# Gate modulation moved under the FFN, attention results in tiles of their own, two FFN result tiles

## The chip, the cores and the metric

The kernel runs on one core of a Trainium2 chip, in one launch. The metric is the device time of that launch in microseconds. Each number given as the kernel's time is the median of several executions. The engines are named as in the profile: PE (TensorE, matrix products), PEld (its weight loads), DVE (VectorE), ACT (ScalarE), POOL (GpSimd) and SP (SyncE, which here only issues DMA transfers). POOL and ACT issue DMA transfers too. Every engine works through its own instruction list in order.

## What is computed

One layer of an encoder, for 512 tokens of 2048 features, in float32:

```python
mod = silu(c) @ w_ada + b_ada                 # c is one row; w_ada is 2048 x 12288
sh1, sc1, g1, sh2, sc2, g2 = split(mod, 6)
h = rms_norm(x, norm1_w) * (1 + sc1) + sh1
qa, ka, va, qb, kb, vb, ga, gb = split(h @ w_in)
ya = global_gqa(rope(rms(qa)), rope(rms(ka)), va)     # 8 heads of 128
yb = neighbourhood_attention(qb, kb, vb, rpb)         # 8 heads of 128
merged = sigmoid(ga) * (ya @ w_oa) + sigmoid(gb) * (yb @ w_ob)
x = x + g1 * (merged @ w_out)
h2 = rms_norm(x, norm2_w) * (1 + sc2) + sh2
ff = (silu(h2 @ w_gate) * (h2 @ w_up)) @ w_down       # 5632 wide
x = x + g2 * ff
out = rms_norm(x, final_w)
```

`mod` is what this document calls the modulation. The part for the first norm (`sh1`, `sc1`) is made at the very start. The rest is made in the background: `sh2` and `sc2`, the first gate `g1` and the second gate `g2`. The first gate is wanted after `w_out`, `sh2` and `sc2` at the second norm, and the second gate only near the end, after `w_down`.

## The kernel before

**Products.** Each float32 operand is split into a rounded part and a remainder (`split`, L165: ACT makes the first on L167, DVE the second on L169), and one product is three matmuls (`mm3`, L187 to L189). Weights come in units of 512 KB: SP loads a unit into a `raw` buffer (`unit`, L194), ACT and DVE split it into a `whl` buffer, and PE reads that. There are four `raw` buffers and three `whl` buffers in pool `wp`, and in some stages one or two more of each in pool `wq`.

**Forms.** `form1` (L248) multiplies with the weights stationary, `form2` (L268) with the tokens stationary. The gates of the attention, its values and the FFN use `group7` (L730): seven products in place of eight for a block, over sums and differences that DVE makes (`wforms`, L674, with the lines 684 to 687). One `group7` handles four units of weights (`s`), in the order 2, 3, 0, 1, and ends with sums out of the accumulators (L762 to L771).

**Order of work.** Stages follow one another: norm and first projections; global attention (`att_a`, with products for gates between); `sg_b` gates and values by `group7`; neighbourhood attention (`att_b`); gates `sg_b` 4 to 7; the products with `w_oa`, `w_ob` and `w_out`; second norm; FFN (11 rounds of `group7` with `w_gate` and `w_up`); the product with `w_down`; final norm. A scheduler then orders each engine's instructions by the order in which the program wrote them and by when their buffers come free in its own model.

**Background work.** After each unit of weights the program calls `pump` (L220). It runs what is due in `soon` (a list of functions, each with a number of pumps to wait), takes one function from `later`, and one step from each of `bg` and, at a pace, `mods`. The pace is `pace["rate"]` steps for each call of `slot` (L214), of which there are two a unit in `form1` and `form2`.

**A block of modulation** is one generator of `mods`, made by `ada_acc` (L367). It has 16 steps. In each step `fetch` (L353) issues loads of 512 KB of `w_ada` into `mw` tiles (three buffers; L357) and DVE adds the loaded tile, times one column of silu(c), into `acc` (L377 for the first step, L379 for the others). These DVE instructions are made with `behind`, which keeps them at the place where the program wrote them. After the last step, `row_sum` (L388) splits a half of `acc`, `row_products` adds its 128 rows up by two matmuls with ones (L396), and `keep` copies the result out (L400) and stores it to DRAM (L401). For `sh2` and `sc2` (`ada_mod`) the stored row is loaded again in columns (L414) and added to its bias by `ada_done` (L363 to L365). For a gate (`ada_gate`) the row stays in DRAM until `rows` spreads it over the partitions.

There are eight blocks, 128 loads. In the kernel before, one block (columns 0 to 3 of `sh2`, `sc2`) runs under the global attention in a pool of its own, `p_w0`, with one `acc` tile. Four run between the neighbourhood attention and the end of the `w_oa` products, in `p_w`. The last three (half of the first gate and the second gate) run under `w_ob` and `w_out`, in `p_w2`; from `w_out` on their loads are issued by SP instead of POOL. `finish` (L230) takes all steps that are left, and empties `soon`.

**Attention results.** Each head's result is written by ACT to a tile `yo` of pool `aside` (tag `y`, two buffers) and stored to DRAM (`y_d`). `attended` (L1041) loads it again by SP (L1042) and splits it. Before, the load goes to a `raw` buffer.

**FFN results.** `c_tile` (L1260) hands out three tiles of 2048 columns in turn, one in pool `ca` and two in `c_p`; in each round, one holds the result with `w_gate` and one that with `w_up`. Their product is stored to `ff_d` by SP.

Of the kernel before, what the change touches and what calls it, by code (L numbers as in the profile page):

```python
# [14 lines left out]
F32 = mybir.dt.float32  # L15
F32R = mybir.dt.float32r
# [4 lines left out]
P = 128  # L21
WARM = 12, 14
D = 2048
T = 512
NT = T // P
KT = D // P
# [86 lines left out]
def encoder_block(ctx: ExitStack, tc, xp, xT, c, ada1_w, ada2_w, b_ada, norm1_w, w_in, q_norm_w, k_norm_w, bias,  # L113
# [28 lines left out]
    def raw_tile(name="raw"):  # L142
        return buffer("raw", [P, 1024], F32, wbufs["raw"], name)
# [86 lines left out]
    def finish():  # L230
        while fetched or mod["next"] < mod["end"]:
            advance(mods)
        pace["rate"] = 0.0
        flush()

    def flush():
        while bg or soon:
            pump()
# [107 lines left out]

    mod = {"pool": None, "queue": nc.gpsimd, "next": 0, "end": 112}

# [4 lines left out]
    def fetch():  # L353
        while mod["pool"] and len(fetched) < 3 and mod["next"] < mod["end"]:
            n = mod["next"]
            w = mod["pool"].tile([P, 1024], F32, tag="mw", name="mw", bufs=3)
            mod["queue"].dma_start(w, ada2_w[n * P:(n + 1) * P, :])  # L357
            fetched.append(w)
            mod["next"] += 1
# [28 lines left out]
    def row_sum(acc, q, tag, dst, then=None):  # L388
        hl = [mod["pool"].tile([P, 512], F32R, tag="acc" + t, name="acc" + t, bufs=1) for t in "hl"]
        split(*hl, acc[:, q * 512:(q + 1) * 512], pin=behind)  # L390
        soon.append((2, lambda: row_products(hl, tag, dst, then)))

    def row_products(hl, tag, dst, then):
        y = bank(tag)
        for n, t in enumerate(hl):
            behind(nc.tensor.matmul(y, ones_r, t, start=n == 0, stop=n == 1))  # L396

        def keep():
            o = io.tile([P, 512], F32, tag="io", name="ada_o")
            behind(V.tensor_copy(o[0:1, :], y[0:1, :]))  # L400
            nc.gpsimd.dma_start(dst, o[0:1, :])  # L401
            if then:
                then()

        soon.append((2, keep))

# [15 lines left out]

    def ada_gate(col, dst):
        return ada_acc(col, lambda acc: soon.extend((1 + q, functools.partial(row_sum, acc, q, "YT"[q], dst[q]))
                                                    for q in range(2)))

# [407 lines left out]
    q1 = [st(F32) for _ in range(NT)]  # L834
    p_w = tc.alloc_tile_pool(name="p_w0", bufs=1, side="right")
    mod.update(pool=p_w, end=16, accs=1)
    mods.append(ada_mod(0, (s2, b_sc2, n2, t2, b_sh2)))
    pace["rate"] = 0.45
    form2(w_in, QA + 512, hT, lambda i, b: S.activation(q1[i], b, AF.Copy))
# [51 lines left out]
    gates(sg_a, GA, 12, 16)  # L891
    finish()
    for h in range(4):
        att_a(4 + h, q, h, 1)
    p_w.release()
    p_a.release()
# [83 lines left out]
    p_w = tc.alloc_tile_pool(name="p_w", bufs=1, side="right")  # L980
    mod.update(pool=p_w, end=80, accs=2)
    mods.extend(ada_mod(k, (s2, b_sc2, n2, t2, b_sh2)) for k in range(4, KT, 4))
    g1_d, g2_d = ([dram.tile([1, 512], F32, name=f"g{n}d{q}") for q in range(4)] for n in (1, 2))
    mods.extend(ada_gate(c * D + q * 512, dst[q:]) for c, dst in ((2, g1_d), (5, g2_d)) for q in (0, 2))
    fetch()
# [54 lines left out]

    def attended(hl, h, yr):  # L1041
        nc.sync.dma_start(yr, y_d[h])  # L1042
        split(*hl, yr)
# [19 lines left out]
    yT, ya = ([pair(p, f"y{k}", T, 1) for k in range(8)] for p in (p_y, p_ya))  # L1063
    later.extend(lambda h=h: attended(ya[h], h, raw_tile("yr")[:, :T]) for h in range(8))
    gates(sg_b, GB, 4, 8)
# [22 lines left out]
    turn = itertools.cycle(("mm", "mm", "S"))  # L1088
    later.extend([lambda: None] * 3 + [lambda h=h: attended(yT[h], 8 + h, raw_tile("yr")[:, :T]) for h in range(8)])
    for j in range(0, KT, 2):  # L1090
# [4 lines left out]
    p_w2 = tc.alloc_tile_pool(name="p_w2", bufs=1, side="left", reuse_waits="tile")  # L1095
    mod.update(pool=p_w2, end=128)
    pace["rate"] = 0.7
    mx, mT = [], []
# [96 lines left out]

    pace["rate"] = 0.6
    for cc in range(2):
        w_out_pass(cc, range(NT))
    pace["rate"] = 0.35
    for cc in (2, 3):  # L1200
# [59 lines left out]
    def c_tile(dt=F32, name="c"):  # L1260
        n = next(cn) % 3
        c = (c_p if n else ca).tile([P, 2048], dt, tag=f"c{n}", name=name, bufs=1)
        return c, c.rearrange("p (a t q n) -> p a t q n", a=2, t=2, q=2)
# [9 lines left out]
    def first_pairs():  # L1273
        early[0] = ff_pair(0, 0, [wq.tile([P, 1024], F32R, tag="ta", name=f"e0{t}", bufs=2) for t in "hl"], nc.sync)
        e1, _ = c_tile(F32R, "e1")
        early[1] = ff_pair(0, 1, [e1[:, :1024], e1[:, 1024:]], nc.sync)

    for n in range(FU):
        cs = []
        for w in (w_gate, w_up):  # L1280
# [8 lines left out]
            def wsrc(s):  # L1289
                d = wforms(w, 4 * s, n * 512)  # L1290
                if s == 1 and n == FU - 1 and w is w_up:
                    first_pairs()
                return d
# [333 lines left out]
```

## Time and profile before

| What | Value |
|---|---|
| Runs | 2507.35, 2507.85 and 2514.26 us; median 2507.85 |
| The profiled execution's own time | 2507.35 us |
| Its span, first to last instruction | 2505.6 us, mean granted clock 0.994 |
| DMA over the span | 461.77 MB, mean 184 GB/s |
| Loads of `mw` issued by POOL | 105, 512 KB each, median 5.2 us to landing |
| Loads of `mw` issued by SP | 23, 512 KB each, median 4.8 us to landing |
| First and last start of the DVE sums of L379 | 255.1 and 1145.9 us |

How to read the rows that follow. A row of waits says who waited, for whom, how long in total, how often, and the longest wait. A row of a stretch (two times with a colon) gives its length, then for PE, PEld, DVE, ACT and POOL the busy time with the number of instructions in brackets, then PE's granted clock as a share of full speed, the busy share of the DMA engines, and GB/s. A row of the timeline gives start, duration, engine, line, operation, output and inputs with their shapes, the number of instructions merged, and in square brackets the engine's idle time ahead of it with what ended that. `SPq` is SP's instruction queue. Names such as `mm`, `S`, `T` and `Y` are accumulator banks; `issue` means that nothing in the profile shows what was waited for.

### The profile page before, as it was taken

The numbers are of one execution on the slowest core, as the hardware profiler recorded it, in microseconds if no ns is written. First come the engines' busy times: TensorE is split into PE (matmuls) and PEld (weight loads), VectorE is DVE, ScalarE is ACT, GpSimd is POOL, SyncE is SP. The second block draws the span as 40 slices with busy tenths as digits, with TensorE's granted clock in tenths as the row PEclk, the third lists the DMA queues.
The fourth block names the chain that finished last, engine by engine and source line by source line (L and its number), as shares of the span: only waits on it lengthen the run. The fifth ranks groups of instructions, "written<-read, shape, count | busy, mean of one in ns | idle before, by whom it ended". The sixth has DMA issues, their size and how long they took to land.

```text
span 2505.6 us, 42099 instructions
## 1 busy us (share of the span) xinstructions
PE 2452.3 (98%) x17183; PEld 2284.5 (91%) x17183; DVE 1992.1 (80%) x2675; ACT 1064.8 (42%) x1462; POOL 148.1 (6%) x247
## 2 busy tenths in 40 slices
PE   8999999999999999999999999999999999999998
PEld 7888788999888788888999999999999998999997
DVE  8985888986677668758798888888888885677877
ACT  5223545443344333236754444444444454434333
POOL 0100000000111112111000000000000000000010
PEclk9999999999999999999999999999999999999999
DMA  9865442345765879788453444443444456547563
GB/s 359 307 235 160 151 143 76 115 142 190 230 212 181 282 251 316 245 295 262 131 160 102 140 131 124 137 128 106 140 127 128 134 185 204 199 138 250 186 239 130
DMA packets 215267, 461.77 MB, mean 184 GB/s; under 512 B 15152, under 2 KB 62624, under 8 KB 206368
## 3 DMA queue, kind: packets, MB, share of 16 engines
q1 hardware_dynamic: 177360, 313.96, 38.9%
q0 software_dynamic: 28720, 128.53, 14.8%
q10 hardware_dynamic: 8992, 16.58, 1.8%
q8 instruction: 135, 2.21, 0.4%
q14 instruction: 60, 0.49, 0.1%
HBM read 412.84 MB, written 46.17 MB: 183 GB/s over the span
## 4 chain that ended last, share of the span: by engine, by line
PE 62%; issue 16%; DVE 11%; DMA 6%; ACT 2%; POOL 1%; DVEq 0%; POOLq 0%; ACTq 0%; SPq 0%
PE mm L189 12%; PE mm L187 12%; PE mm L188 12%; PE S L189 5%; PE S L188 5%; PE S L187 5%; PE Y L188 2%; PE Y L187 2%; PE Y L189 2%; DVE whl L169 2%; DVE raw L514 2%; DMA raw<-in_w_down 2%; DMA mw<-in_ada_w 1%; DVE acc L379 1%; DMA g<-sga 1%
## 5 line engine op out<-in xcount | busy, mean ns | idle before, releaser
L167 ACT ACTIVATE whl<-raw 128x1024 fp32r<-128x1024 f32 (+1 forms) x483 | 455.0, 946 | 664.7 <-PE mm L189 275.8
L169 DVE TENSOR_TENSOR whl<-raw,whl 128x1024 fp32r<-128x1024 f32 (+1 forms) x483 | 521.2, 1089 | 149.2 <-ACT whl L167 148.6
L169 DVE TENSOR_TENSOR whl<-ta,whl 128x1024 fp32r<-128x1024 f32 x120 | 146.6, 1221 | 73.0 <-ACT whl L167 72.8
L167 ACT ACTIVATE whl<-tb 128x1024 fp32r<-128x1024 f32 x120 | 127.5, 1062 | 173.7 <-PE S L189 116.7
L167 ACT ACTIVATE whl<-ta 128x1024 fp32r<-128x1024 f32 x120 | 127.0, 1059 | 169.3 <-PE mm L189 112.3
L379 DVE SCALAR_TENSOR_TENSOR acc<-mw,cact,acc 128x1024 f32<-128x1024 f32 x124 | 159.2, 1284 | 22.9 <-DMA mw<-in_ada_w 22.1
L169 DVE TENSOR_TENSOR whl<-tb,whl 128x1024 fp32r<-128x1024 f32 x120 | 146.3, 1219 | 8.4 <-ACT whl L167 7.3
L684 DVE TENSOR_TENSOR ta<-raw 128x512 f32<-128x512 f32 x120 | 82.7, 689 | 40.1 <-DMA raw<-in_w_down 37.6
L685 DVE TENSOR_TENSOR ta<-raw,ta 128x512 f32<-128x512 f32 x120 | 82.5, 687 | 34.6 <-DMA raw<-in_w_down 28.9
L357 POOL DMA_DIRECT2D mw<-in_ada_w x105 | 56.2, 536 | 708.1 <-DVE acc L379 299.2
L187 PE MATMUL mm<-x56h,whl 128*128 128x256 f32 x336 | 92.4, 275 | 0.0
L188 PE MATMUL mm<-x56l,whl 128*128 128x256 f32 x336 | 92.4, 275 | 0.0
L189 PE MATMUL mm<-x56h,whl 128*128 128x256 f32 x336 | 92.4, 275 | 0.0
L188 PE MATMUL mm<-whl,s 128*128 128x256 f32 x320 | 88.2, 276 | 1.1 <-DVE whl L169 1.0
L187 PE MATMUL mm<-whl,s 128*128 128x256 f32 x320 | 88.1, 275 | 0.0
L187 PE MATMUL mm<-x3h,whl 128*128 128x256 f32 x320 | 88.0, 275 | 0.0
L188 PE MATMUL mm<-x3l,whl 128*128 128x256 f32 x320 | 88.0, 275 | 0.0
L189 PE MATMUL mm<-x3h,whl 128*128 128x256 f32 x320 | 88.0, 275 | 0.0
L187 PE MATMUL S<-x56h,whl 128*128 128x256 f32 x320 | 88.0, 275 | 0.0
L188 PE MATMUL S<-x56l,whl 128*128 128x256 f32 x320 | 88.0, 275 | 0.0
L189 PE MATMUL S<-x56h,whl 128*128 128x256 f32 x320 | 88.0, 275 | 0.0
L189 PE MATMUL mm<-whl,s 128*128 128x256 f32 x320 | 88.0, 275 | 0.0
(1822 smaller groups left out, 8874.8 us busy)
## 6 DMA issues: line engine op xcount, KB each, us to landing
raw<-in_w_in SPq DMA_DIRECT2D x133, 512.0 KB, 4.4
mw<-in_ada_w POOLq DMA_DIRECT2D x105, 512.0 KB, 5.2
raw<-in_w_gate SPq DMA_DIRECT2D x92, 512.0 KB, 4.0
raw<-in_w_up SPq DMA_DIRECT2D x88, 512.0 KB, 3.8
raw<-in_w_down SPq DMA_DIRECT2D x88, 512.0 KB, 5.6
raw<-in_ada_w POOLq DMA_DIRECT2D x29, 1024.0 KB, 6.9
raw<-in_w_out SPq DMA_DIRECT2D x48, 512.0 KB, 5.4
mw<-in_ada_w SPq DMA_DIRECT2D x23, 512.0 KB, 4.8
```

What stands on the lines that cost most here:

```text
L167: high = pin(S.activation(hi, src, AF.Copy))
L169: latest[:] = [high, pin(eng.tensor_sub(lo, src, hi))]
L187: nc.tensor.matmul(o, lh, rh, start=start, stop=False, **kw)
L188: nc.tensor.matmul(o, lh, rl, start=False, stop=False, **kw)
L189: nc.tensor.matmul(o, ll, rh, start=False, stop=stop, **kw)
L357: mod["queue"].dma_start(w, ada2_w[n * P:(n + 1) * P, :])
L379: behind(V.scalar_tensor_tensor(acc, part, cact[:, k:k + 1], acc, op0=ALU.mult, op1=ALU.add))
L514: V.scalar_tensor_tensor(raw, raw, 1.0, call, op0=ALU.mult, op1=ALU.mult, accum_out=y)
L684: V.tensor_sub(t1, b12, b11)
L685: V.tensor_sub(t2_, b22, t1)
```

## The change

One block fewer runs early and two run late. No modulation is made under the global attention: the pool `p_w0` goes. The four blocks of the next stretch (64 loads) are now columns 0 to 7 and the whole first gate. The two blocks under `w_ob` and `w_out` (32 loads) are columns 8 to 15, at a pace of 0.5 in place of 0.7, 0.6 and 0.35. The second gate's two blocks (32 loads) run under the FFN, from its second round on: four steps a round, one after the weights of each second and third unit of a `group7`, with one `mw` buffer, one `acc`, and the splits of the row sums in `io` tiles; four empty steps follow each block.

The load in `attended` goes to a tile of pool `aside` instead of a `raw` buffer, and begins one pump later after the neighbourhood attention. `c_tile` hands out two tiles instead of three; the room of the third holds the new `mw` and `acc`.

```diff
-    mod = {"pool": None, "queue": nc.gpsimd, "next": 0, "end": 112}
+    mod = {"pool": None, "queue": nc.gpsimd, "next": 0, "end": 0, "accs": 2, "loads": 3}
     def fetch():
-        while mod["pool"] and len(fetched) < 3 and mod["next"] < mod["end"]:
-            n = mod["next"]
-            w = mod["pool"].tile([P, 1024], F32, tag="mw", name="mw", bufs=3)
+        while mod["pool"] and len(fetched) < mod["loads"] and mod["next"] < mod["end"]:
+            n = mod["next"] + {2: 32, 3: 32, 4: -32, 5: -32}.get(mod["next"] // KT, 0)
+            w = mod["pool"].tile([P, 1024], F32, tag="mw", name="mw", bufs=mod["loads"])
     def row_sum(acc, q, tag, dst, then=None):
-        hl = [mod["pool"].tile([P, 512], F32R, tag="acc" + t, name="acc" + t, bufs=1) for t in "hl"]
+        few = mod["loads"] == 1
+        hl = [io.tile([P, 512], F32R, tag="io", name="acc" + t) if few else
+              mod["pool"].tile([P, 512], F32R, tag="acc" + t, name="acc" + t, bufs=1) for t in "hl"]
         split(*hl, acc[:, q * 512:(q + 1) * 512], pin=behind)
-        soon.append((2, lambda: row_products(hl, tag, dst, then)))
+        soon.append((1 if few else 2, lambda: row_products(hl, tag, dst, then)))
...
-    p_w = tc.alloc_tile_pool(name="p_w0", bufs=1, side="right")
-    mod.update(pool=p_w, end=16, accs=1)
-    mods.append(ada_mod(0, (s2, b_sc2, n2, t2, b_sh2)))
-    pace["rate"] = 0.45
     form2(w_in, QA + 512, hT, lambda i, b: S.activation(q1[i], b, AF.Copy))
...
-    finish()
+    flush()
     for h in range(4):
         att_a(4 + h, q, h, 1)
-    p_w.release()
...
     p_w = tc.alloc_tile_pool(name="p_w", bufs=1, side="right")
-    mod.update(pool=p_w, end=80, accs=2)
-    mods.extend(ada_mod(k, (s2, b_sc2, n2, t2, b_sh2)) for k in range(4, KT, 4))
+    mod.update(pool=p_w, end=64)
-    mods.extend(ada_gate(c * D + q * 512, dst[q:]) for c, dst in ((2, g1_d), (5, g2_d)) for q in (0, 2))
+    mods.extend(columns_of((0, 4)))
+    mods.extend(gate_of(2, g1_d))
+    mods.extend(columns_of((8, 12)))
+    for half_gate in gate_of(5, g2_d, "TT"):
+        mods.extend((half_gate, iter([None] * 4)))
...
-    def attended(hl, h, yr):
+    def attended(hl, h):
+        yr = aside.tile([P, T], F32, tag="y", name="yr")
         nc.sync.dma_start(yr, y_d[h])
         split(*hl, yr)
...
-    later.extend(lambda h=h: attended(ya[h], h, raw_tile("yr")[:, :T]) for h in range(8))
+    later.append(lambda: None)
+    later.extend(lambda h=h: attended(ya[h], h) for h in range(8))
...
-    mod.update(pool=p_w2, end=128)
-    pace["rate"] = 0.7
+    mod.update(pool=p_w2, end=96)
+    pace["rate"] = 0.5
...
-    pace["rate"] = 0.6
     for cc in range(2):
         w_out_pass(cc, range(NT))
-    pace["rate"] = 0.35
     for cc in (2, 3):
         w_out_pass(cc, (0, 1))
...
     def c_tile(dt=F32, name="c"):
-        n = next(cn) % 3
+        n = next(cn) % 2
...
-        e1, _ = c_tile(F32R, "e1")
-        early[1] = ff_pair(0, 1, [e1[:, :1024], e1[:, 1024:]], nc.sync)
+        early[1] = ff_pair(0, 1, [c_p.tile([P, 1024], F32R, tag=t, name="e1", bufs=1) for t in ("mw", "acc")], nc.sync)
+    mod.update(pool=c_p, queue=nc.gpsimd, end=128, accs=1, loads=1)
     for n in range(FU):
...
                 d = wforms(w, 4 * s, n * 512)
+                if n and s % 3 == 0:
+                    advance(mods)
                 if s == 1 and n == FU - 1 and w is w_up:
+                    finish()
                     first_pairs()
```

More of the change, by code (lines that the diff above doesn't have):

```diff
@@ L403, in keep @@
                 then()
-        soon.append((2, keep))
+        soon.append((1 if mod["loads"] == 1 else 2, keep))
     def ada_mod(k0, to):
@@ L421, in ada_mod, with ada_gate @@
         return ada_acc(None, done)
-    def ada_gate(col, dst):
-        return ada_acc(col, lambda acc: soon.extend((1 + q, functools.partial(row_sum, acc, q, "YT"[q], dst[q]))
-                                                    for q in range(2)))
+    def ada_gate(col, dst, tags):
+        return ada_acc(col, lambda acc: soon.extend((1 + q * (4 if mod["loads"] == 1 else 1),
+                                                     functools.partial(row_sum, acc, q, tags[q], dst[q])) for q in range(2)))
     def rows(dst, src):
@@ L980, in encoder_block @@
     p_w = tc.alloc_tile_pool(name="p_w", bufs=1, side="right")
-    mod.update(pool=p_w, end=80, accs=2)
-    mods.extend(ada_mod(k, (s2, b_sc2, n2, t2, b_sh2)) for k in range(4, KT, 4))
+    mod.update(pool=p_w, end=64)
     g1_d, g2_d = ([dram.tile([1, 512], F32, name=f"g{n}d{q}") for q in range(4)] for n in (1, 2))
-    mods.extend(ada_gate(c * D + q * 512, dst[q:]) for c, dst in ((2, g1_d), (5, g2_d)) for q in (0, 2))
+    columns_of = lambda ks: (ada_mod(k, (s2, b_sc2, n2, t2, b_sh2)) for k in ks)
+    gate_of = lambda c, dst, tags="YT": (ada_gate(c * D + q * 512, dst[q:], tags) for q in (0, 2))
+    mods.extend(columns_of((0, 4)))
[3 more added lines that the diff above has]
+        mods.extend((half_gate, iter([None] * 4)))
     fetch()
@@ L1088, in encoder_block @@
     turn = itertools.cycle(("mm", "mm", "S"))
-    later.extend([lambda: None] * 3 + [lambda h=h: attended(yT[h], 8 + h, raw_tile("yr")[:, :T]) for h in range(8)])
+    later.extend([lambda: None] * 3 + [lambda h=h: attended(yT[h], 8 + h) for h in range(8)])
     for j in range(0, KT, 2):
```

## The prediction

> **What bounds the kernel now.** I read the page's busy times first, then the busy time and clock of single stretches, then PE's waits stage by stage, then the order of instructions around the longest waits.
>
> ```profile
> PE 2452.3 (98%) x17183; PEld 2284.5 (91%) x17183; DVE 1992.1 (80%) x2675; ACT 1064.8 (42%) x1462; POOL 148.1 (6%) x247
> 1000.00:1036.00 36.00, 36.00 (x168) 31.46 (x167) 26.13 (x34) 11.29 (x15) 3.61 (x6) 1.00 0.54 175
> 1305.10:1380.10 75.00, 75.00 (x674) 75.00 (x673) 64.35 (x81) 33.18 (x35) 0.00 (x0) 1.00 0.40 124
> 250.00:260.00 10.00, 7.09 (x27) 5.71 (x26) 7.84 (x18) 1.44 (x2) 2.49 (x5) 0.83 0.88 309
> 390.00:400.00 10.00, 9.11 (x49) 8.29 (x50) 6.69 (x17) 5.40 (x12) 0.00 (x0) 0.83 0.08 28
> 827.00:840.00 13.00, 9.92 (x30) 7.37 (x29) 11.04 (x13) 6.64 (x10) 3.23 (x6) 0.74 0.91 324
> 1050.00:1060.00 10.00, 6.96 (x18) 4.99 (x17) 8.08 (x8) 1.06 (x1) 2.13 (x4) 0.68 0.93 346
> ```
>
> PE is busy 98% of the span, and no matmul is taken away. The time can fall only where PE waits or runs slowed. Undisturbed, 168 matmuls of 512 columns fill 36.0 us, 0.214 us each. In the FFN PE is busy for all of 75.0 us while DVE has 10.65 us free. The last four rows are the bad places: 30 matmuls in 13 us are 30 x 0.214 = 6.4 us of work, so 6.6 us are lost there; likewise 10 - 18 x 0.214 = 6.1 us at 1050 and 10 - 27 x 0.214 = 4.2 us at 250. The clock in them is 0.68 to 0.83: a wait costs itself and then slowed matmuls.
>
> PE's waits (total, times, longest), first from 240 to 480 us:
>
> ```profile
> PE T L804 <- issue: 2.9, 1, 2.9
> PE Y L188 <- DVE ptl L169: 1.8, 1, 1.8
> PE S L187 <- ACT e L856: 1.1, 2, 0.9
> ```
>
> From 640 to 860 us:
>
> ```profile
> PE mm L187 <- ACT whl L167: 3.0, 1, 3.0
> ```
>
> From 860 to 1000 us:
>
> ```profile
> PE mm L189 <- DVE whl L169: 2.3, 4, 0.8
> PE mm L187 <- ACT whl L167: 0.8, 1, 0.8
> ```
>
> From 1000 to 1260 us:
>
> ```profile
> PE mm L187 <- ACT whl L167: 2.6, 1, 2.6
> PE mm L187 <- DVE ro L1145: 1.4, 2, 0.8
> ```
>
> **Part 1: no modulation under the global attention.** Sixteen loads, their DVE sums and one chain of row sums leave 250 to 390 us. The order of instructions shows what they did:
>
> ```profile
> 251.37 0.54 DVE L800 TENSOR_TENSOR rt<-rt,rp 128x128 f32<-128x128 f32 x2
> 251.43 0.38 PE L187 MATMUL mm<-whl,h3h 128*128 128x512 f32 x1
> 253.54 0.76 DVE L377 TENSOR_SCALAR acc<-mw,cact 128x1024 f32<-128x1024 f32 x1 [1.64 <-DMA mw<-in_ada_w]
> 254.20 0.42 DVE L801 TENSOR_TENSOR rt<-rt 128x256 f32<-128x256 f32 x1
> 254.72 0.57 PE L804 MATMUL T<-ident,rt 128*128 128x128 f32 x2 [2.91 <-issue]
> ```
>
> And at 389 us, DVE and then PE:
>
> ```profile
> 389.47 0.16 DVE L364 TENSOR_TENSOR t<-ada_c,vec 128x4 f32<-128x4 f32 x1 [2.15 <-DMA ada_c<-md]
> 390.15 0.68 DVE L169 TENSOR_TENSOR ptl<-T,pth 128x512 fp32r<-128x512 f32 x1
> 390.89 0.38 PE L188 MATMUL Y<-ptl,st 128*128 128x256 f32 x1 [1.83 <-DVE ptl L169]
> ```
>
> Both times DVE, in order, stands on a modulation instruction whose DMA hasn't landed, with the instruction that PE needs behind it. Without it L801 could start when L800 ends (251.9) and the transposes at about 252.4, so about 0.8 us of the first wait stay: 4.2 - 0.8 = 3.4 us won. The second wait, 1.83 us, goes with its slowed stretch (a clock of 0.83 over 10 us withholds 1.7 us): 3.5 us. The 1.1 us on e (L856) come from the same queue and go. Term: 8.0 us. Bounds: 2.9 + 1.8 = 4.7 less 0.8 if the clock is no part of the gain, and 8.8.
>
> **Part 2: attention results in tiles of their own.** L1042 loads no longer take a raw buffer, which the weights use. SP's order, and PE behind it:
>
> ```profile
> 811.13 0.34 SPq L1042 DMA_DIRECT2D yr<-y  x1
> 827.24 0.37 SPq L194 DMA_DIRECT2D raw<-in_w_in  x1
> 831.95 0.80 PE L187 MATMUL mm<-h0h,whl 128*128 128x512 f32 x1 [3.04 <-ACT whl L167]
> ```
>
> SP's waits from 640 to 1000 us:
>
> ```profile
> SPq L1042 <- DVE whl L169: 21.1, 7, 5.4
> SPq L194 <- DVE y0l L169: 17.1, 2, 15.7
> ```
>
> The weight load at 827.24 stood up to 15.7 us for a raw buffer that an attention result held, and PE waited 3.04 us for it. With four raw buffers for weights alone, it can start before 811 us. But the two y tiles also hold the last heads' outgoing results, so the first y load now waits for those stores, each later one for the split two before it, and what SP issues behind them waits too. I take 5 of the 6.6 us, and 1.5 of the 3.1 us of small waits from 860 to 1000 us. Bounds: -3 (those small waits double) and 9.7.
>
> **Part 3: 16 loads fewer from 950 to 1150 us.** The pace there falls from 0.7, 0.6 and 0.35 to 0.5, and the stretch carries 32 loads where it carried 48. SP's order:
>
> ```profile
> 1042.39 0.45 SPq L194 DMA_DIRECT2D raw<-in_w_out  x1
> 1044.33 8.44 SPq L357 DMA_DIRECT2D mw<-in_ada_w  x3
> ```
>
> The loads issued from 1030 to 1060 us (count, size, median us to landing):
>
> ```profile
> mw<-in_ada_w SPq DMA_DIRECT2D x7, 512.0 KB, 5.1
> mw<-in_ada_w POOLq DMA_DIRECT2D x4, 512.0 KB, 4.7
> x<-in_xp SPq DMA_DIRECT2D x2, 1024.0 KB, 8.6
> raw<-in_w_out SPq DMA_DIRECT2D x2, 512.0 KB, 8.6
> ```
>
> The weights took 8.6 us (median) beside eleven loads for the modulation and two of 1 MB; DMA is at 0.93. At the new pace (one load per unit of 24 x 0.214 = 5.1 us) some six of the eleven remain, 2.5 MB less; but all four pieces of the first gate, ready earlier, now come into the same stretch. I take half of the 6.1 us: 3. The first residual (L1145, 1.4 us) waits less, since its gate is there: 0.7. Against this, the last two column blocks end later: by the pace the 32nd load comes in the second pass over w_out, and their chain of stores, loads and sums (the one that cost 3.5 us at 389) ends one unit ahead of the second norm. I charge 1. Term: 2.7; bounds -3.5 (the chain waits once, nothing else gains) and 7.5.
>
> **Part 4: 32 loads and sums under the FFN.** The price of one sum, how its load landed (min/median/max), and the narrowest place of the FFN's weights:
>
> ```profile
> L379 DVE SCALAR_TENSOR_TENSOR acc<-mw,cact,acc x124: 1264/1280/1692, 255.1 to 1145.9; 128x1024 f32<-128x1024 f32 x124
> DMA to landing us min/median/max: 3.4/5.1/9.2
> 1377.33 1.82 DVE L169 TENSOR_TENSOR whl<-raw,whl 128x512 fp32r<-128x512 f32 x2
> 1380.33 0.28 PE L189 MATMUL mm<-m6h,whl 128*128 128x256 f32 x1
> ```
>
> 32 x 1.28 = 41 us of DVE. Two group products take 75 us and get four sums, 5.1 us, out of 10.65 free: the free time covers them. The lead matters as well: after an up group DVE has finished the next weights some 2.3 us before PE reads them (the first of two ending near 1378.0, read at 1380.33). The sums stand behind the second and third unit, not at this place; even both together, 2.56 us, would pass it by 0.3 us. One buffer for the load suffices: two sums are at least one unit of 75/8 = 9.4 us apart, and the load takes 5.1. The matmuls of the row sums (eight here, 0.214 us each) are only moved. POOL has nothing queued in this stretch (x0 above). The two result tiles instead of three cost nothing: each is rewritten 75 us later. Term: 0; bounds +1 and -10 x 0.3 - 4 = -7 (a late load at each half gate included).
>
> **The sum.** 8.0 + 5 + 1.5 + 2.7 + 0 = 17.2 us, against the profiled execution's own 2507.35 us (span 2505.6): 2490.2. That execution is 0.5 us below the median of the three runs, 2507.85. I predict 2490.
>
> The slowed matmuls are a large part of it. The clock of 0.83 after 389 follows a wait of only 1.83 us. The Trainium skill, "TensorE: Matmul & The Clock Gate", Part 1, says that the clock is halved after an idle window of some 3.4 us; none of the waits above is that long. By that rule the four places would be worth their waits alone (2.9, 1.8, 3.0 and 2.6 us), and with the same shares the sum would be some 10 us, 2497. The rows of this trace contradict it, and I keep them.
>
> **Rivals.**
> - Given back near by: the gain under the global attention holds, but the weights meet the y loads and the x and gate loads instead, and 827 and 1050 stay; the chain before the second norm costs its 3.5 us. 8 - 3.5 = 4.5 won: 2503. For it: DMA is at 0.91 and 0.93 there, and the scheduler's order will be another. Against: 16 loads and the raw buffers are really gone. 0.2.
> - The waits under the attention aren't the modulation's: DVE then waits for the rope or for softmax instead, and only the 1.1 and 1.5 us go. 2505. Against: both rows name the DMA. 0.08.
> - Slower: two y tiles throttle SP. Fourteen of the sixteen y loads wait for the split two before; if each then costs PE the 0.8 us that is the longest small wait above, that is 11 us, and two slowed stretches 2 x 3.4 more; less 8.0 it ends at 2517. It decides from about 0.6 us a load on. For it: SP already waited 21.1 us at L1042. Against: the y loads waited for splits before as well, those rows say so. 0.06.
> - Slower: the load under the FFN is late, and DVE, in order, stands on it at every group. 20 groups x (2.56 + 1 - 2.3) = 25 us, less 17: 2515 and more. Against: 5.1 us of load in 9.4. 0.05. The Trainium skill, "SBUF — State Buffer", SBUF: two separate sides, says that POOL can be kept from writing its descriptors by some DVE copies; POOL's loads here landed in 5.1 us under a busy DVE, so no row shows it.
>
> **How the numbers follow.** The forecast has 0.61 and its own range, 2481 to 2499: all of the waits (8.8 + 9.7 + 7.5 = 26 won) to half of the sum. The whole range, 2479 to 2509, takes in the first two rivals with some 4 us on top, and 2 us below for waits shorter than those listed; it leaves out the slow rivals. A measurement of this kernel tells about 0.3% from no change, 2500.3 to 2515.4. Faster: 0.60 from the forecast, 0.08 from the first rival and 0.02 from the second: 0.70. Same: 0.01 + 0.12 + 0.06 = 0.19. Slower: 0.11, the last two.
>
> **What would show it.** No DVE wait on mw or ada_c ahead of 600 us, and PE's waits of 2.9 and 1.8 us gone; the weight load of the first gates after the local attention ahead of 820 us; a w_out load near 1042 landing in under 8 us; PE still busy 75.0 of 75.0 us in the FFN with DVE near 69.5. Wrong would be: PE waits on whl in the FFN; SP waiting longer at the y loads than before, with PE waits of over 1 us between 830 and 1000 us; a DVE wait on ada_c near 1140 us.

## The result, and the profile after

The changed kernel takes 2485.94 us (median of four runs, 2482.74 to 2488.69) where the kernel before, run beside it, took 2507.6: a ratio of 0.9911, 95% interval 0.9885 to 0.9937. On a second chip it took 2480.3 us (six runs, 2476.42 to 2485.19) against 2504.34: 0.9898, 0.9881 to 0.9916. The forecast was 2490, its own range 2481 to 2499; the second chip's median lies 1 us below that range, within the whole range of 2479 to 2509.

The profiled execution took 2482.74 us, its span 2481.0. The line of the page with the busy times:

```profile
PE 2440.6 (98%) x17183; PEld 2275.9 (92%) x17183; DVE 1990.0 (80%) x2675; ACT 1064.2 (43%) x1462; POOL 154.5 (6%) x258
```

Busy time and clock of single stretches (PE, PEld, DVE, ACT and POOL busy, with the number of instructions; then the granted clock, the DMA share and GB/s):

```profile
250.00:260.00 10.00, 8.64 (x42) 7.01 (x42) 7.38 (x20) 2.77 (x4) 0.00 (x0) 1.00 0.46 155
390.00:400.00 10.00, 10.00 (x62) 8.35 (x61) 7.81 (x20) 6.03 (x13) 0.00 (x0) 1.00 0.07 27
...
845.00:865.00 20.00, 16.52 (x66) 12.90 (x65) 12.89 (x18) 8.29 (x13) 1.06 (x2) 0.91 0.84 259
...
1050.00:1060.00 10.00, 10.00 (x48) 8.73 (x47) 5.11 (x6) 2.11 (x2) 0.02 (x1) 1.00 0.95 332
...
1405.00:1480.00 75.00, 75.00 (x674) 75.00 (x674) 68.38 (x85) 33.16 (x36) 2.11 (x4) 1.00 0.49 156
```

The same matmuls take 11.7 us less of PE's busy time than before: that is slowed time that has gone. Three of the four bad places ran undisturbed or nearly so; the fourth has moved from 827 to 859 us (66 matmuls in 20 us are 14.1 us of work). From 1405 to 1480 us, in the FFN, PE is busy for all of 75.0 us, with four sums on DVE.

PE's waits by stretch (total, times, longest), from 240 to 480, 640 to 860, 860 to 1000 and 1000 to 1260 us:

```profile
PE mm L189 <- DVE whl L169: 1.9, 2, 1.3
PE T L806 <- issue: 1.3, 1, 1.3
...
PE mm L187 <- ACT whl L167: 2.4, 1, 2.4
PE mm L189 <- DVE whl L169: 1.8, 2, 1.2
...
PE mm L187 <- ACT whl L167: 1.4, 1, 1.4
...
PE mm L189 <- DVE whl L169: 0.9, 1, 0.9
```

To see where time went I added up PE's work in each trace, in columns multiplied, and took the moments at which every kernel had started as much of it as before at seven places; the differences are the stretches. The row sums of the modulation count as work, so a row sum that runs in another stretch makes neither of the two longer by itself. The stretches are named by the time at which they end in the first profile of before; all values are us of one profiled execution. ffn_out has eight row-sum matmuls less, so its last two values are not at the same place as the others'.

```
                    start  global att.  local att.  gates+w_oa  w_ob+w_out  FFN     w_down
                    to 57  57-503       503-823     823-1000    1000-1255   -2110   -2496
before               56.8   446.1        320.0       176.9       255.1       855.1   385.6
before, again        56.0   444.0        320.6       179.5       259.0       854.8   380.6
after                60.0   433.2        319.4       177.4       245.2       856.0   379.6
after, again         56.7   433.6        319.3       175.0       245.2       856.2   378.6
ga_back              55.5   443.1        319.0       170.9       245.2       855.9   379.2
ga_y_back            55.7   448.9        319.3       176.8       245.2       855.9   379.5
y_back               56.5   432.9        319.4       177.4       245.2       855.9   384.3
pace_old             59.0   433.3        319.3       177.8       245.2       855.9   384.3
order_half           62.2   433.2        319.4       174.1       250.0       856.0   379.4
half_back            56.8   433.3        319.4       177.8       251.3       857.2   379.6
pace_up              57.6   434.2        321.6       175.9       245.2       856.1   379.7
yg                   60.4   432.7        319.4       177.5       245.2       856.7   382.8
ffn_out              59.9   433.7        319.4       178.9       245.2       854.7   379.0
sums4                57.7   433.3        319.3       175.9       245.2       907.9   384.4
```

Mean of two profiles each, after less before: start +2.0, global attention -11.7, local attention -0.9, first gates and w_oa -2.0, w_ob and w_out -11.9, FFN +1.1, w_down -4.0. The first and the last stretch differ by as much between runs of one kernel, so the change is two gains of 12 us each, and little else that is clear of this scatter. The lower rows are the experiments.

### The profile page after: what moved, and what is told of

The parts are those of the page before. It is cut to its first block, busy times and chain, and to the rows that moved or that the text cites. A ratio compares the mean times of both kernels' runs of the same rounds, so it can differ in the third digit from the quotient of the medians.

```text
span 2481.0 us, 42040 instructions
## 1 busy us (share of the span) xinstructions
PE 2440.6 (98%) x17183; PEld 2275.9 (92%) x17183; DVE 1990.0 (80%) x2675; ACT 1064.2 (43%) x1462; POOL 154.5 (6%) x258
## 4 chain that ended last, share of the span: by engine, by line
PE 75%; DVE 12%; issue 6%; DMA 3%; ACT 1%; POOL 0%; DVEq 0%; POOLq 0%; ACTq 0%; SPq 0%
PE mm L189 15%; PE mm L188 15%; PE mm L187 15%; PE S L187 6%; PE S L188 6%; PE S L189 6%; PE Y L187 3%; PE Y L188 3%; PE Y L189 3%; DVE whl L169 3%; DVE raw L516 2%; DMA raw<-in_w_down 1%; PE T L874 1%; PE T L189 1%; PE T L188 1%
## 5 line engine op out<-in xcount | busy, mean ns | idle before, releaser
L357 POOL DMA_DIRECT2D mw<-in_ada_w x116 | 61.8, 533 | 1407.9 <-DVE acc L379 850.8
L687 DVE TENSOR_TENSOR ta<-raw,ta 128x512 f32<-128x512 f32 x120 | 82.7, 689 | 58.2 <-DMA raw<-in_w_down 28.4
```

Of the source, the lines that this page charges most:

```text
L687: V.tensor_sub(t2_, b22, t1)
```

## The experiments

**The column block back under the global attention (ga_back).** It undoes part 1 alone; 48 loads instead of 64 are then left for the stretch from 503 to 960 us (before had 64 there too).

```diff
+    p_w = tc.alloc_tile_pool(name="p_w0", bufs=1, side="right")
+    mod.update(pool=p_w, end=16, accs=1)
+    mods.append(ada_mod(0, (s2, b_sc2, n2, t2, b_sh2)))
+    pace["rate"] = 0.45
...
-    mods.extend(columns_of((0, 4)))
+    mods.extend(columns_of((4,)))
```

> The changed kernel (2485.9 us) with its first column block put back under the global attention: 16 loads, their sums and one chain of row sums at 250 to 390 us, and 48 instead of 64 loads under the local attention. Theory A (the waits and slowed stretches of 250 to 470 us were the modulation's, some 14 us by the place-by-place difference of the two traces): 2497 to 2501 us, with DVE waits on mw or ada_c ahead of 400 us. The prediction's term was 8.0 us: 2494. Theory B (the gain there came from another order of instructions or from luck of the run): within 3 us of 2486.

Measured: 2485.64 us (2480.68 to 2492.0), ratio to before 0.9927 (0.9905 to 0.9949); the changed kernel, on other chips, has 0.9911 and 0.9898. By its time that is theory B; by its trace it is theory A. PE's waits from 240 to 480 us are those of before again:

```profile
PE T L806 <- issue: 2.8, 1, 2.8
PE mm L187 <- ACT whl L167: 2.5, 1, 2.5
PE Y L188 <- DVE ptl L169: 2.1, 1, 2.1
PE S L187 <- ACT e L858: 1.6, 2, 1.5
```

The stretch takes 443.1 us, 10 more than the 433.2 and 433.6 of the changed kernel. The four profiles with the modulation there have 443.1 to 448.9, the ten without it 432.7 to 434.2, and in each of the four the wait on the weight split near 450 us (second row) is 2.5 us; in each of the ten it is gone, and one of 1.24 to 1.27 us comes some 18 us later. So all these waits come and go with the modulation, and the second row is one that the prediction had left out. But that one is of another kind: the last modulation instruction on DVE runs at 389 us in before, some 60 us ahead of it. What differs there is the order of instructions. DVE in before, where ACT and then PE wait for the second row:

```profile
447.50 1.22 DVE L169 TENSOR_TENSOR s27l<-sb,s27h 128x1024 fp32r<-128x1024 f32 x1
448.64 0.68 DVE L685 TENSOR_TENSOR ta<-raw,ta 128x512 f32<-128x512 f32 x1
```

And in the changed kernel, where L687 is the same line of the program:

```profile
438.08 0.69 DVE L687 TENSOR_TENSOR ta<-raw,ta 128x512 f32<-128x512 f32 x1
...
439.28 1.22 DVE L169 TENSOR_TENSOR s27l<-sb,s27h 128x1024 fp32r<-128x1024 f32 x1
```

For this wait theory B's "another order of instructions" holds; why the modulation changes the order so far behind it was not tried. Further on, the kernel gained 4 to 6.5 us in the first gates and w_oa (170.9 us in its one profile, no PE wait at all from 860 to 1000 us), where it has 16 loads fewer than the changed kernel. About half of what part 1 gains where it takes loads away is paid where those loads must go instead.

**The heads' results in raw buffers again (y_back).** It undoes part 2 alone.

```diff
-    def attended(hl, h):
-        yr = aside.tile([P, T], F32, tag="y", name="yr")
+    def attended(hl, h, yr):
...
-    later.extend(lambda h=h: attended(ya[h], h) for h in range(8))
+    later.extend(lambda h=h: attended(ya[h], h, raw_tile("yr")[:, :T]) for h in range(8))
```

> The changed kernel with the heads' results loaded into raw buffers again, as before. Theory A (the tiles of their own moved the wait from 828 us to 859 and 918 us and are worth nothing in sum): 2484 to 2488 us, with the wait of about 3 us near 828 us back and the ones at 859 and 918 us gone or smaller. The prediction's term for them was 6.5 us: 2492.5. Theory B (they even cost something): 2480 to 2483.

Measured: 2483.45 us (2479.59 to 2485.27), 0.9912 (0.9891 to 0.9932). The stretch takes 177.4 us, as in the changed kernel (177.4 and 175.0). The time lies between the ranges of the two theories and far from the 2492.5 of the prediction's term; and theory A's wait of 3 us near 828 us did not come back either. SP's waits from 640 to 1000 us in this kernel:

```profile
SPq L194 <- DVE y0l L169: 8.1, 1, 8.1
```

The weights' wait for a buffer held by an attention result is 8.1 us here, where it was 15.7 us in before: what made it long was not the shared buffers alone.

**The old pace (pace_old).** 0.7, 0.6 and 0.35 loads a unit from w_ob on, with 32 loads.

```diff
-    pace["rate"] = 0.5
+    pace["rate"] = 0.7
...
+    pace["rate"] = 0.6
     for cc in range(2):
         w_out_pass(cc, range(NT))
+    pace["rate"] = 0.35
```

> The changed kernel with the old pace of the modulation from w_ob on (0.7, 0.6 and 0.35 loads per unit instead of 0.5), still with 32 loads there. Theory A (the stretch near 1050 us was won because loads no longer crowd the first weights of w_out; by the old pace a good part of them comes back there): 2489 to 2494 us, a w_out load near 1042 us landing in over 7 us. Theory B (it was won because 16 loads and one block of columns are gone from the stretch, whatever the pace): 2484 to 2488. The prediction gave 3 us to the pace and the fewer loads together.

Measured: 2484.97 us (2483.01 to 2486.51), 0.9921 (0.9901 to 0.9941). The stretch takes 245.2 us, to the tenth what it takes at the new pace. The loads of w_out issued from 1015 to 1050 us did land late (count, size, median us to landing):

```profile
raw<-in_w_out SPq DMA_DIRECT2D x8, 512.0 KB, 8.2
```

That is theory A's sign without its cost, since PE's longest wait from 1000 to 1260 us is 0.7 us. Theory B: the pace is worth nothing.

**Half of the second gate back in w_ob and w_out (half_back).** 48 loads there, at the old pace.

```diff
-    for half_gate in gate_of(5, g2_d, "TT"):
-        mods.extend((half_gate, iter([None] * 4)))
+    halves = list(gate_of(5, g2_d))
+    mods.append(halves[0])
...
-    mod.update(pool=p_w2, end=96)
+    mod.update(pool=p_w2, end=112)
...
+    mods.append(ada_gate(5 * D + 1024, g2_d[2:], "TT"))
```

> The kernel with the old pace (2485.0 us), and one half of the second gate's modulation back in the products with w_ob and w_out: 48 loads there as before the change, 16 under the FFN. Theory A (the 7 to 10 us of that stretch were won by the fewer loads): 2490 to 2495 us, and PE waits of over 2 us near 1045 us again. Theory B (they were won by the order of the pieces, the first gate ahead of two blocks of columns, whatever the number): 2484 to 2487.

Measured: 2492.3 us (2487.47 to 2493.72), 0.9942 (0.9926 to 0.9959), beside the changed kernel on the same chip at 2480.3 (0.9898, 0.9881 to 0.9916): 12 us slower, and the intervals lie apart. Six of them are in this stretch (251.3 for 245.2 us), one in the FFN; the rest lies in stretches that scatter. Theory A's time, but not its place: nothing waits for over 0.8 us near 1045. PE's longest wait, 1.9 us, comes later (waits from 1060 to 1180 us):

```profile
PE mm L187 <- DVE ro L1149: 2.8, 2, 1.9
```

DVE's order there:

```profile
1099.40 1.27 DVE L379 SCALAR_TENSOR_TENSOR acc<-mw,cact,acc 128x1024 f32<-128x1024 f32 x1
1100.60 1.21 DVE L169 TENSOR_TENSOR whl<-raw,whl 128x1024 fp32r<-128x1024 f32 x1
1101.73 1.27 DVE L379 SCALAR_TENSOR_TENSOR acc<-mw,cact,acc 128x1024 f32<-128x1024 f32 x1
1102.93 1.27 DVE L1149 TENSOR_TENSOR ro<-mm,gate 128x512 f32<-128x512 f32 x2
```

With 48 loads, sums still run when the first pass over w_out ends (1101 us), and the residual that frees PE's banks stands behind two of them.

**The old order, with 32 loads (order_half).** The first gate's second half is modulated behind the start of w_ob, as before, and the third column block ahead of it; old pace.

```diff
-            n = mod["next"] + {2: 32, 3: 32, 4: -32, 5: -32}.get(mod["next"] // KT, 0)
+            n = mod["next"] + {3: 16, 4: 16, 5: -32}.get(mod["next"] // KT, 0)
...
-    mods.extend(columns_of((0, 4)))
+    mods.extend(columns_of((0, 4, 8)))
     mods.extend(gate_of(2, g1_d))
-    mods.extend(columns_of((8, 12)))
+    mods.extend(columns_of((12,)))
```

> The kernel with the old pace (2485.0 us), with the first gate's second half modulated behind the start of w_ob's products, as before, and the third column block ahead of it; 32 loads there either way. Theory A (the wait of 2.6 us at 1045 us before and its slowed stretch, 6.6 us, came from the gate's row sums and first sums of the next half standing on DVE ahead of a weight split, which set SP's next weight load back by 10.9 us; so the order of the pieces is what won it): a wait of over 2 us near 1035 to 1045 us and residual waits, 2490 to 2495 us. Theory B (it needs the number of loads, 48): 2484 to 2487.

Measured: 2487.18 us (2480.62 to 2493.59), 0.9935 (0.9917 to 0.9952): by the times 2 us from pace_old, which is within the scatter. The trace decides: the stretch takes 250.0 us for 245.2, and PE waits again:

```profile
PE mm L188 <- DVE whl L169: 2.5, 2, 1.7
```

DVE's order in before, from 1029 us:

```profile
1031.15 0.68 DVE L169 TENSOR_TENSOR accl<-acc,acch 128x512 fp32r<-128x512 f32 x1
1031.76 1.28 DVE L379 SCALAR_TENSOR_TENSOR acc<-mw,cact,acc 128x1024 f32<-128x1024 f32 x1
...
1035.09 1.28 DVE L379 SCALAR_TENSOR_TENSOR acc<-mw,cact,acc 128x1024 f32<-128x1024 f32 x1
...
1036.62 1.22 DVE L169 TENSOR_TENSOR whl<-raw,whl 128x1024 fp32r<-128x1024 f32 x1
```

In order_half:

```profile
1019.39 0.69 DVE L169 TENSOR_TENSOR accl<-acc,acch 128x512 fp32r<-128x512 f32 x1
...
1028.28 1.28 DVE L379 SCALAR_TENSOR_TENSOR acc<-mw,cact,acc 128x1024 f32<-128x1024 f32 x1 [0.94 <-DMA mw<-in_ada_w]
1029.48 1.22 DVE L169 TENSOR_TENSOR whl<-raw,whl 128x1024 fp32r<-128x1024 f32 x1
```

And in the changed kernel:

```profile
1022.40 1.22 DVE L169 TENSOR_TENSOR whl<-raw,whl 128x1024 fp32r<-128x1024 f32 x1
1023.54 1.28 DVE L379 SCALAR_TENSOR_TENSOR acc<-mw,cact,acc 128x1024 f32<-128x1024 f32 x1
```

In the first two, the gate's row sum and three (before) or five sums (order_half) stand ahead of the weights' split in DVE's order, between the last products of w_ob and the first of w_out. In before ACT had its half of this split ready at 1030.45 us and DVE began its own at 1036.62; the row sum's split and the three sums take 4.2 of those 6.2 us. SP stood 10.9 us in all for the buffer that the split frees (order_half shows the late split, not that long wait on SP). Theory A, then, in its mechanism, though both its time of 2490 to 2495 and its wait of over 2 us stayed away: the order brings back 4.8 us of the 11.9, without residual waits (0.4 us); the number of loads brings another 6.1 us elsewhere.

**The FFN without the modulation (ffn_out).** The call that advances the modulation between the FFN's weights is taken out, with the 32 loads; the kernel leaves the second gate's own values out and uses the first gate's.

```diff
-                if n and s % 3 == 0:
-                    advance(mods)
```

> The changed kernel without the second gate's modulation: its 32 loads, sums and row sums under the FFN are left out (the first gate's values stand in for the second's). Theory A (DVE's free time under the FFN covers all of it): 2484 to 2488 us, PE busy 75.0 of 75.0 us in the FFN in both, and the stage of w_down as in the changed kernel. Theory B (the sums cost PE small waits that the trace misses, or loads that shift w_down's first weights): 2479 to 2483.

Measured: 2478.29 us (2475.16 to 2482.76), 0.9891 (0.9865 to 0.9917). The FFN takes 854.7 us for 856.0 and 856.2. In that time PE also does 1.7 us more of the other work, in place of the eight row-sum matmuls (8 x 0.214), so the same work takes 3.0 to 3.2 us less. What is left of that beside the 1.7, 1.3 to 1.5 us, is mostly one wait: PE's 0.9 us for a weight split that the changed kernel has at 1243 us (the last row of its waits above) and that neither profile of before has, nor this kernel. DVE's order in the changed kernel there:

```profile
1241.50 1.28 DVE L379 SCALAR_TENSOR_TENSOR acc<-mw,cact,acc 128x1024 f32<-128x1024 f32 x1
1242.70 1.22 DVE L169 TENSOR_TENSOR whl<-tb,whl 128x1024 fp32r<-128x1024 f32 x1
```

The first sum of the second gate stands ahead of the split, 44 us before the next one; every kernel with this modulation waits 0.7 to 1.1 us there. The other sums and the loads cost PE no wait. The whole kernel came out below both theories' figures, but 0.9891 and 0.9898 are no different.

**Each sum four times (sums4).**

```diff
-                behind(V.scalar_tensor_tensor(acc, part, ...))
+                for _ in range(4 if mod["loads"] == 1 else 1):
+                    behind(V.scalar_tensor_tensor(acc, part, ...))
```

> The changed kernel with each of the 32 sums under the FFN made four times (the second gate's modulation counts each product four times): 5.1 us of DVE a step instead of 1.28. Theory A (what hides the sums is DVE's free time, 10.65 us per 75 us): DVE needs 64.35 + 4 x 5.1 = 84.8 us per pair of groups with four steps, eight such pairs, so 8 x 9.8 = 78 us more, 2560 to 2570 us, DVE near 100% busy there. Theory B (the lead ahead of PE counts, and each wait brings a slowed stretch): 2575 to 2620. If DVE runs ahead far enough in the groups without sums, under 2540.

Measured: 2535.54 us in its one run; the FFN takes 907.9 us, 52 more. PE's longest waits in the FFN, in total, then a stretch with ten sums and two with 16 each:

```profile
PE mm L189 <- DVE whl L169: 25.0, 20, 2.6
```

```profile
1255.00:1330.00 75.00, 72.01 (x641) 71.50 (x640) 70.95 (x87) 31.18 (x34) 1.05 (x2) 1.00 0.42 136
1405.00:1480.00 75.00, 71.66 (x633) 70.76 (x632) 75.00 (x89) 30.81 (x33) 2.11 (x4) 1.00 0.43 148
1480.00:1555.00 75.00, 70.75 (x623) 69.83 (x622) 75.00 (x88) 30.05 (x32) 2.13 (x4) 1.00 0.42 141
```

In the last two DVE is full and PE does 628 of its 674 matmuls in 75 us, so a pair of groups takes 75 x 674 / 628 = 80.5 us and not the 84.8 of theory A. There the price of a sum was wrong, not the mechanism. In the changed kernel four sums of 1.28 raise DVE's busy time from 64.35 to 68.38, by 4.0 and not by 5.1: the next instruction starts 1.20 us after a sum (rows 1241.50 and 1242.70 above); why four of them add still less was not followed. With 64.35 + 16 x 1.0 = 80.4 the 80.5 comes out. But eight such pairs are 44 of the 52 us, and in the first stretch PE falls short by 33 matmuls while DVE still has 4 us free. So sums in bunches of four cost PE time before DVE is full, as the first half of theory B had it, the lead ahead of PE; its second half, slowed matmuls behind the waits, did not come (granted clock 1.00 in all three rows). The time, under 2540 us, is that of the expectation's last case, but DVE doesn't run ahead here: it is full.

**The loads under the local attention faster (pace_up).**

```diff
-    later.extend([lambda: None] * 4 + [lambda: pace.update(rate=0.55)])
+    later.extend([lambda: None] * 4 + [lambda: pace.update(rate=0.8)])
```

> The changed kernel with 0.8 instead of 0.55 loads per unit under the local attention, so that the 64 loads there are nearly done when the attention outputs' product (820 to 960 us) begins. Theory A (what the 16 added loads cost in that stage took back most of the gain under the global attention: the kernel with them put back gained 6.9 us between 823 and 1000 us, the changed one nothing): the waits at 859 and 918 us go, 2478 to 2481 us. Theory B (the waits there come from the heads' results and the gates' own loads, which ACT stands on, whatever else is loaded): 2484 to 2488. Against both: DVE at 0.75 busy under the local attention gets about 16 x 1.28 = 20 us more there; if PE waits for it, over 2488.

Measured: 2487.92 us (2481.81 to 2492.22), 0.9924 (0.9905 to 0.9943). The waits at 859 and 918 us did go, but two on DVE's half of a split, 6.3 us, came at 834 and 846 us:

```profile
PE mm L189 <- DVE whl L169: 6.3, 2, 4.0
```

175.9 us in the stretch, and 2.3 more under the local attention. Nothing won: theory A's gain doesn't come.

**Results and gates loaded ahead into tiles of their own (yg).**

```diff
-        yr = aside.tile([P, T], F32, tag="y", name="yr")
+        yr = p_y.tile([P, T], F32, tag="o", name="yr", bufs=4)
...
+        gs = [aside.tile([P, T], F32, tag="go", name="g") for _ in range(2)]
+        for j in range(2):
+            nc.gpsimd.dma_start(gs[j], src[j])
...
-            g = io.tile([P, T], F32, tag="io", name="g")
-            nc.sync.dma_start(g, src[j])
+            g = gs[j]
```

> The changed kernel with four tiles instead of two for the heads' results on their way in, apart from those on their way out, and with the gates of the attention outputs loaded a group ahead into tiles of their own by GpSimd's queue, so that ACT no longer stands on either load. Theory A (ACT in order, standing on y and g loads with the weights' splits behind it, makes the waits of 2.4 us at 859 and 1.4 us at 918 us): both go, 2478 to 2482 us. Theory B (the weights' own loads are late in the crowd of 800 to 960 us): the waits stay under another name, 2484 to 2488.

Measured: 2485.09 us (2477.75 to 2488.4), 0.991 (0.9889 to 0.9931); 177.5 us in the stretch. Theory B: the two waits go, and others come (from 820 to 900 us):

```profile
PE T L398 <- ACT acch L167: 2.4, 1, 2.4
PE mm L187 <- ACT whl L167: 2.2, 3, 1.3
```

**Both parts undone (ga_y_back).** The two edits of ga_back and y_back together.

> The changed kernel with two parts undone: a column block's modulation back under the global attention, and the heads' results back in raw buffers. Against the kernel with only the first undone (2485.6 us; between 823 and 1000 us of before it gained 6.9 us, with 48 loads there instead of 64). Theory A (tiles of their own do bring the 6.5 us of the prediction when the stretch isn't crowded by 16 more loads): the 6 to 7 us are lost again, 2491 to 2494 us, with a wait of 2 to 3 us near 820 us. Theory B (the 16 loads fewer alone made that gain): 2484 to 2488 us.

Measured: 2493.1 us (2488.05 to 2497.12), 0.9955 (0.9938 to 0.9971), 7.5 us above ga_back. The time is theory A's, and so is the stretch (176.8 for 170.9), but its cause is not. (The profiled execution lost another 5.8 us under the global attention, where the two kernels have the same text.) PE's one long wait there, at 839 us, SP's longest wait, and SP's order ahead of it:

```profile
PE mm L187 <- ACT whl L167: 8.9, 1, 8.9
```

```profile
SPq L1089 <- DMA g1d<-ada_o: 14.0, 1, 14.0
```

```profile
816.63 15.29 SPq L1089 DMA_DIRECT2D g<-sga  x3
832.27 0.38 SPq L194 DMA_DIRECT2D raw<-in_w_in  x1
```

SP stood 14.0 us at a gate's load, whose tile still held a row of the modulation on its way out, and the first gates' weights came behind it. No raw buffer is in that. What the tiles of their own are worth by themselves stays open.

**The kernel before once more (before_again).**

> The kernel before once more, for a second profile. 2500 to 2510 us. If the waits belong to the kernel: 2.9 us at 254, 1.8 at 391, 2.5 at 448, 3.0 at 832 and 2.6 near 1045 us, as in the first profile. The w_down stage tells whether the changed kernel's 6 us there are its own: the first profile has waits of 1.8, 1.0 and 1.0 us at 2133, 2194 and 2266 us; if they are missing here, that gain is run noise, and it will be 0 to 3 us against this profile.

Measured: 2506.32 us, one run. The waits under the global attention are there again (2.6, 1.9 and 2.5 us), so is the one near 830 (3.1) and the one in w_out (2.9 us, at 1054); the three in w_down are not. The 5 us between its two w_down stretches is as much as the changed kernel seemed to gain there.

## Why the prediction was right

The median, 2485.94, lies 4 us below the forecast and in its own range. The sum was 17.2 us and the runs show 22 to 24. That it came so near is in part luck: the terms were off by more, in both directions, and two of them (parts 1 and 3) came out above their own upper bounds.

**Part 1** (8.0, at most 8.8): 11.7 by the trace. The two waits named went as said; at the transposes behind the rope (L806) 1.3 us stayed (1.7 in the second profile) where 0.8 was left. The failed step is the list of waits: the weight split on ACT near 450 us, 2.5 us and its slowed matmuls behind it, was not in it. It is there in every profile with the modulation and in none without, by another order of instructions and not by a modulation instruction ahead of it. And the loads taken away were counted as gone: ga_back shows that they cost 4 to 6.5 us where they now run, so the part by itself is worth some 4 to 7 us and not its 10 to 12.

**Part 2** (6.5): 2.0 at most by the two pairs of profiles; y_back, with raw buffers, takes as long as the first of them. The step on SP held: the last weight load of the first gates is issued at 800.02 us, where it was 827.24.

```profile
800.02 0.37 SPq L194 DMA_DIRECT2D raw<-in_w_in  x1
```

What failed is that PE's wait was put down to the buffer alone. Where 64 loads run, PE waits for some split behind a load or a sum on ACT or DVE, whichever was mended here: the stretch takes 174 to 180 us in every kernel but ga_back, with 48 loads and tiles of their own.

**Part 3** (2.7, at most 7.5): 11.9. The mechanism was wrong in the main, not just the size. The slow landing of the weights, 8.6 us beside eleven loads, was read as the cause of the wait at 1050. After the change the weights land 1.7 us sooner, beside six, as the prediction's sign had it (loads issued from 1030 to 1060 us):

```profile
raw<-in_w_out SPq DMA_DIRECT2D x8, 512.0 KB, 6.9
mw<-in_ada_w SPq DMA_DIRECT2D x6, 512.0 KB, 4.8
```

and the stretch moves 335 GB/s without a wait of PE. But pace_old's weights take 8.2 us and PE waits for none, so a landing that slow is not by itself the cause of a wait. The load at 1042 us was issued late: the one ahead of it had stood 10.9 us for a buffer, with the sums on DVE ahead of the split that frees it. A row of SP's waits (L194 on whl) and the order on DVE would have told. How much of the 2.6 us is the late issue and how much the landing was not separated. The other half of the gain, the residual behind DVE, was priced at 0.7 from waits of 1.4 us; order (4.8 us) and number (6.1 us) of the loads each bring about half of the 11.9. The last columns' chain, charged at 1 us, did come: DVE waits 3.9 us on ada_c at 1132 us, which the prediction named as a sign of being wrong. PE had its next work by then and lost nothing.

```profile
DVE t L364 <- DMA ada_c<-md: 4.6, 2, 3.9
```

**Part 4** (0): right to about 1 us. The FFN is 1.1 us longer, by the one wait on whl at 1243 us; PE waits on whl in the FFN were named as a sign of being wrong. At the narrow place that the prediction looked at, PE waits for nothing. sums4 shows that DVE's free time is what hides four sums in a pair of groups, and that ten, in bunches of four, no longer hide.

**The rivals.** "Given back near by" is partly what happened: from 823 to 1000 us at most 2.0 of the 6.5 us are left. It lost by part 3, which gained what the other two fell short of. Of the slower rivals, that of the two y tiles showed its mechanism at one place. ACT's order ahead of PE's wait at 859 us:

```profile
855.66 0.63 ACT L167 ACTIVATE y3h<-yr 128x512 fp32r<-128x512 f32 x1 [5.22 <-DMA yr<-y]
...
858.03 1.04 ACT L167 ACTIVATE whl<-raw 128x1024 fp32r<-128x1024 f32 x1
```

ACT stands 5.2 us on a y load that came late, with the weights' split behind it, and PE waits 2.4 us (1.1 in the second profile). The prediction had named SP's longer waits at the y loads, with PE waits of over 1 us behind 830 us, as a sign of being wrong. The PE waits came; SP's waits at the y loads hardly grew, from 35.9 to 37.0 us. And yg shows that with four tiles the stretch is no shorter. The loads under the FFN were in time. The rule of the clock, by which the sum would have been 2497, is spoken of below.

## What to carry to other kernels

When a wait falls together with a crowded DMA, look at when the late load was issued and what held its queue before putting it down to bandwidth: here SP stood 10.9 us at a load, behind a split that three sums and a row sum's split had set back by 4.2 us. Background work moves well to a stretch where the engine that does it has free time and PE never waits (the FFN, but for one sum placed ahead of its first splits); moved to a stretch that already has waits it is paid again there. And several terms that touch the same queue don't add: undo them one by one and together before believing any one price.

## What the runs showed that was not expected

One wait doesn't have one price. The waits recur at the same places with the same length, but the slowed matmuls after them don't. Eight or ten us from the end of a wait, in the first profile of before:

```profile
450.40:460.40 10.00, 9.93 (x64) 9.93 (x65) 10.00 (x15) 3.57 (x5) 0.00 (x0) 0.71 0.33 105
...
832.00:840.00 8.00, 7.96 (x21) 6.00 (x22) 6.56 (x7) 2.07 (x3) 2.53 (x5) 0.59 1.02 383
```

And in the second:

```profile
448.70:458.70 10.00, 9.95 (x75) 9.95 (x76) 10.00 (x15) 3.83 (x4) 0.00 (x0) 0.84 0.34 105
...
829.80:837.80 8.00, 7.44 (x26) 5.97 (x27) 6.57 (x7) 2.11 (x3) 2.46 (x5) 0.79 1.02 387
```

Behind a wait of 2.50 and 2.51 us PE did 64 matmuls in one execution and 75 in the other; behind 3.04 and 3.14 us, 21 and 26. Over the fourteen profiles, matmuls at half their pace follow waits of 1.1 to 8.9 us for 2 to 6 us, and after others of the same length not at all: after 2.85 us at 253 us in ga_back nothing, after 2.58 us at the same place in the second profile of before 3.5 us; and in the FFN of sums4, after waits of up to 2.6 us, hardly any. So the tail of a wait cost anything from 0 to some 3 us here, and two of the prediction's four tails, read from one execution, were the longer of two (4.7 us for 2.6 behind 832 us, 5.1 for 3.4 behind 1054 us). The slowest and the fastest run of one kernel lie 3.5 to 17 us apart; these tails, of which one execution has a handful, are a likely part of that, but that was not tried by itself. The Trainium skill, "TensorE: Matmul & The Clock Gate", Part 1, says that the window in which the idleness is judged runs freely. A tail that depends on the moment agrees with that; that it takes an idle window of 3.4 us does not, since most of these waits were shorter.

The second is the price of a sum on DVE: 1.28 us by its row, 1.20 us from its start to the next instruction's, and 1.0 us by what four of them add to DVE's busy time.
